# Unit 0 of a rotary embedding kernel: smaller rows for its first half, and GpSimd's queue for its second

## The chip, the cores and the metric

The kernel runs on one core of a Trainium2 chip. The metric is the device time of one execution in microseconds (us). A run more than 1.5% above the fastest of its kernel is called slow. All comparisons below are between the others, called fast, unless a text says otherwise. A profile is one execution, and its span is shorter than its measured time by a nearly constant 1.7 to 1.8 us, so traces are compared with traces and times with times. The profiled execution of the kernel before took 84.54 us (span 82.8 us), which is above its median of 84.26 us, so a difference of a few tenths of a us can't be read from two spans.

## The reference, cut to what matters

```python
angles = np.outer(positions * scale, freqs)
cos, sin = np.cos(angles), np.sin(angles)
x_first, x_second = x[:, :, :, :half], x[:, :, :, half:]      # x: (8, 8, 1024, 64) float32
out_first = x_first * cos - x_second * sin
out_second = x_first * sin + x_second * cos
```

Input and output are 16.8 MB each. Whatever the kernel does, it moves 33.6 MB.

## The kernel before

The 64 heads are worked in four units of 16 heads. A unit is 128 partitions of 32 KB, 4 MB in HBM. GpSimd issues the loads, which cast float32 to float16 on the way; only a quarter of unit 0 is loaded by SyncE, without a cast. VectorE rotates in place in float16, half a unit at a time, ScalarE casts the half to a float32 tile OUT, and OUT is stored. `FIRST` cuts the first half of unit 0 into stores with rows of 4, 4 and 8 KB per partition. A row is what a store takes from one partition; in the traces each row is one packet, and a store's 128 rows are spread over sixteen DMA engines, eight on each.

```python
FIRST = (0, NH // 4, NH // 2, NH)          # NH = 4096 elements, 16 KB: half a unit's row
xout = ctx.enter_context(tc.tile_pool(name="xout", bufs=3))
...                                         # loads of X0..X3 from GpSimd, sine and cosine tables
for u in range(NU):
    OUT = xout.tile([P, N], FP32, tag="O")
    for s in range(2):
        ...                                 # four VectorE instructions on X[u], in place
        pin(nc.scalar.copy(out=OUT[:, ns], in_=Xf[u][:, ns]))
        if u in (0, NU - 1):
            eng = nc.gpsimd if (u, s) == (NU - 1, 0) else nc.sync
            cuts = FIRST if (u, s) == (0, 0) else (ns.start, ns.stop)
            for a, b in zip(cuts, cuts[1:]):
                pin(eng.dma_start(out=ov[u][:, a:b], in_=OUT[:, a:b]))
    if u not in (0, NU - 1):
        pin(nc.gpsimd.dma_start(out=ov[u], in_=OUT))
```

## Time and profile before

| | kernel before |
|---|---|
| time, median | 84.26 us (3 runs, 84.17 to 84.31) |
| span of the profile | 82.8 us |
| busy: VectorE, ScalarE, GpSimd | 60.3, 38.5, 5.2 us |
| DMA engines, mean share from 2.0 to 81.2 us | 1.00 |
| last instruction of VectorE, last cast of ScalarE end | 69.8 us, 73.5 us |
| last store issued, landed | 73.5 us, 81.9 us |

To read it: an engine with 73% of the span (VectorE) looks like the bound, and it is not. What matters is that the sixteen DMA engines are busy throughout from 2.0 to 81.2 us (mean share 1.00). The page's list of DMA issues shows who issues what (KB of each, then median us from issue to landing):

```profile
out_dram<-OUT POOLq DMA_DIRECT2D x2, 4096.0 KB, 14.7
...
out_dram<-OUT SPq DMA_DIRECT2D x2, 2048.0 KB, 18.0
...
out_dram<-OUT SPq DMA_DIRECT2D x2, 512.0 KB, 17.6
out_dram<-OUT SPq DMA_DIRECT2D x1, 1024.0 KB, 23.0
```

SyncE (SP) stores unit 0 in two stores of 512 KB, one of 1 MB and one of 2 MB, and the last half of unit 3. GpSimd (POOL) stores units 1 and 2 and the first half of unit 3. A store of 512 KB alone would take 1.3 us (8 rows of 0.16 us on each engine); that it needs 17.6 us to land tells that it shares every DMA engine with the loads.

### The profile page before, as it was taken

The page shows a single profiled execution, that of the slowest core. Times are in us where ns is not written, and L with a number is a line of the kernel's source. Part 1 is how long each engine was busy: PE and PEld are TensorE (multiplying, and loading weights), DVE is VectorE, ACT ScalarE, POOL GpSimd, SP SyncE. Part 2 cuts the span into 40 slices and gives each one's busy share as a digit, 9 for nine tenths or more (in the row PEclk, how much of TensorE's full clock was granted, in tenths as well). Part 3 has the DMA queues.
Part 4 walks back from the last instruction along what each step waited for, and adds up shares of the span by engine and source line. Part 5 has one row for each costly group of instructions (what it writes and reads, how often), then busy time and mean ns, then how long its engine had stood idle before and what let it go on. Part 6 is the DMA issues. An engine that isn't in the chain of part 4 may idle for free.

```text
span 82.8 us, 181 instructions
## 1 busy us (share of the span) xinstructions
PE 6.5 (8%) x18; PEld 2.6 (3%) x18; DVE 60.3 (73%) x40; ACT 38.5 (47%) x18; POOL 5.2 (6%) x15
## 2 busy tenths in 40 slices
PE   0011798200000000000000000000000000000000
PEld 0011233000000000000000000000000000000000
DVE  0306276999999999999999999999999997000000
ACT  1402259992960691294088049209606912950000
POOL 4920000000000000000000200000100020000000
PEclk9999999997555555555555555555555555555555
DMA  2898997999799799899898999997999899799990
GB/s 44 343 314 190 238 261 158 230 253 214 166 253 245 166 277 230 196 279 253 190 158 360 447 443 420 515 499 309 459 491 428 348 507 459 317 443 420 443 443 8
DMA packets 2018, 25.70 MB, mean 310 GB/s; under 512 B 354, under 2 KB 354, under 8 KB 610
## 3 DMA queue, kind: packets, MB, share of 16 engines
q0 software_dynamic: 1008, 18.35, 75.0%
q1 hardware_dynamic: 864, 7.34, 21.6%
q10 hardware_dynamic: 146, 0.01, 0.1%
HBM read 16.79 MB, written 16.78 MB: 405 GB/s over the span
## 4 chain that ended last, share of the span: by engine, by line
DVE 63%; ACT 7%; DMA 6%; issue 5%; PE 5%; DVEq 1%; ACTq 0%
DVE X L154 22%; DVE pr L153 22%; DVE X L158 10%; DVE X L155 8%; DMA freq_row<-in_freqs_dram 6%; ACT OUT L161 4%; PE ps L129 4%; DVEq L197 1%; ACT T L139 1%; PE cfreq L97 1%; ACT tab L122 1%; DVE r L113 1%; DVE y L104 1%; ACTq L70 0%; ACT tab L117 0%
## 5 line engine op out<-in xcount | busy, mean ns | idle before, releaser
L161 ACT CAST OUT<-X 128x4096 f32<-128x4096 f16 x8 | 28.8, 3605 | 25.8 <-DVE X L158 25.8
L153 DVE TENSOR_TENSOR pr<-X,T 128x4096 f16<-128x4096 f16 x8 | 18.3, 2292 | 1.0 <-ACT T L139 0.7
L154 DVE TENSOR_TENSOR X<-X,T 128x4096 f16<-128x4096 f16 x8 | 18.3, 2292 | 0.3
L155 DVE TENSOR_TENSOR X<-X,pr 128x2048 f16<-128x2048 f16 x8 | 9.8, 1225 | 0.3
L158 DVE TENSOR_TENSOR X<-pr,X 128x2048 f16<-128x2048 f16 x8 | 9.7, 1218 | 0.0
L139 ACT CAST T<-ps 128x1024 f16<-128x1024 f32 x6 | 5.7, 1028 | 2.6 <-PE ps L129 2.6
L129 PE MATMUL ps<-tab,sel 128*128 128x512 f16 x16 | 5.9, 534 | 2.6 <-ACT tab L122 2.2
L168 POOL DMA_DIRECT2D out_dram<-OUT x2 | 1.1, 536 | 54.5 <-ACT OUT L161 54.5
L137 DVE CAST T<-ps 128x1024 f16<-128x1024 f32 x2 | 2.4, 1224 | 2.2 <-PE ps L129 2.2
L95 DVE COPY sel<-one 128x2048 f16<-128x2048 f16 x1 | 0.7, 695 | 2.8 <-POOL one L87 2.8
L117 ACT ACTIVATE tab<-r 128x256 f16<-128x256 f32 x1 | 0.4, 416 | 4.8 <-DVE r L113 4.8
L129 PEld LDWEIGHTS <-sel 128*128 128x128 f16 x16 | 2.1, 130 | 6.0 <-issue 5.6
L117 ACT ACT_TABLE_LOAD x1 | 1.3, 1283 | 1.7 <-issue 1.7
L92 POOL DMA_DIRECT2D X<-in_x_dram x3 | 2.0, 659 | 0.0
L140 ACT CAST X<-X0f 128x2048 f16<-128x2048 f32 x1 | 1.9, 1942 | 0.0
L100 DVE CAST posf<-pos_i 128x8 f32<-128x8 int32 x1 | 0.2, 171 | 2.2 <-DMA pos_i<-in_positions_dram 2.2
L97 PE MATMUL cfreq<-freq_row,coef 1*128 1x32 f32 x2 | 0.6, 390 | 5.9 <-DMA freq_row<-in_freqs_dram 5.9
L166 POOL DMA_DIRECT2D out_dram<-OUT x1 | 0.5, 531 | 6.6 <-ACT OUT L161 6.6
L104 DVE TENSOR_TENSOR y<-posf,cfreq 128x256 f32<-128x256 f32 x1 | 0.4, 421 | 0.7 <-PE cfreq L97 0.7
L83 POOL DMA_DIRECT2D X<-in_x_dram x1 | 0.7, 669 | 0.8 <-POOLq L183 0.8
L97 PEld LDWEIGHTS cfreq<-freq_row,coef 1*128 1x128 f32 x2 | 0.5, 304 | 5.9 <-issue 5.9
L122 ACT ACTIVATE tab<-ra,quarter 128x256 f16<-128x256 f32 x1 | 0.5, 508 | 0.0
(11 smaller groups left out, 2.3 us busy)
## 6 DMA issues: line engine op xcount, KB each, us to landing
out_dram<-OUT POOLq DMA_DIRECT2D x2, 4096.0 KB, 14.7
X<-in_x_dram POOLq DMA_DIRECT2D x3, 2048.0 KB, 29.2
out_dram<-OUT SPq DMA_DIRECT2D x2, 2048.0 KB, 18.0
out_dram<-OUT POOLq DMA_DIRECT2D x1, 2048.0 KB, 10.3
X<-in_x_dram POOLq DMA_DIRECT2D x1, 1536.0 KB, 11.5
X0f<-in_x_dram SPq DMA_DIRECT2D x1, 1024.0 KB, 4.8
out_dram<-OUT SPq DMA_DIRECT2D x2, 512.0 KB, 17.6
out_dram<-OUT SPq DMA_DIRECT2D x1, 1024.0 KB, 23.0
```

Of the source, the lines that this page charges most:

```text
L92: pin(nc.gpsimd.dma_start(out=Xf[u], in_=xv[u]))
L97: nc.tensor.matmul(out=cfreq, lhsT=coef, rhs=freq_row, start=True, stop=True)
L117: pin(nc.scalar.activation(out=tab[:, 0], in_=r, func=AF.Sin, bias=0.0, scale=-_TWO_PI_DN))
L129: nc.tensor.matmul(out=ps[:, i].rearrange("p t w -> p (t w)"), lhsT=sel[:, g + i].rearrange("s h q -> s (h q)"), rhs=tab.rearrange("s t k ...
L137: pin(nc.vector.tensor_copy(out=dst, in_=ps))
L139: pin(nc.scalar.copy(out=dst, in_=ps))
L140: pin(nc.scalar.copy(out=Xf[0][:, N - Q :], in_=X0f[:, :Q]))
L153: pin(nc.vector.tensor_tensor(out=pr, in0=Xs, in1=sin_b, op=ALU.mult))
L154: pin(nc.vector.tensor_tensor(out=Xs, in0=Xs, in1=cos_b, op=ALU.mult))
L155: pin(nc.vector.tensor_tensor(out=Xs[:, :, 0, :], in0=Xs[:, :, 0, :], in1=pr[:, :, 1, :], op=ALU.subtract))
L158: pin(nc.vector.tensor_tensor(out=Xs[:, :, 1, :], in0=pr[:, :, 0, :], in1=Xs[:, :, 1, :], op=ALU.add))
L161: pin(nc.scalar.copy(out=OUT[:, ns], in_=Xf[u][:, ns]))
```

## The change

Its intent is to give SyncE's stores of unit 0 shorter rows, so that they take less of the DMA engines from the loads, and to move half of unit 0 out of SyncE's queue, so that it does not compete with the store of unit 1.

```diff
-    FIRST = (0, NH // 4, NH // 2, NH)
+    C1 = NH // 4
...
-            if u in (0, NU - 1):
-                eng = nc.gpsimd if (u, s) == (NU - 1, 0) else nc.sync
-                cuts = FIRST if (u, s) == (0, 0) else (ns.start, ns.stop)
-                for a, b in zip(cuts, cuts[1:]):
-                    pin(eng.dma_start(out=ov[u][:, a:b], in_=OUT[:, a:b]))
-        if u not in (0, NU - 1):
+            if (u, s) == (0, 0):
+                for c in range(0, NH, C1):
+                    pin(nc.sync.dma_start(out=ov[u][:, c : c + C1], in_=OUT[:, c : c + C1]))
+            if u == NU - 1:
+                eng = nc.sync if s else nc.gpsimd
+                pin(eng.dma_start(out=ov[u][:, ns], in_=OUT[:, ns]))
+        if u == 0:
+            OUT0 = OUT
+        elif u < NU - 1:
             pin(nc.gpsimd.dma_start(out=ov[u], in_=OUT))
+        if u == 1:
+            pin(nc.gpsimd.dma_start(out=ov[0][:, NH:], in_=OUT0[:, NH:]))
```

## The prediction

> **What bounds the kernel now.** I began with the page's chain of work that ended last. It names VectorE for 63% of the span, and it ends at the last cast on ScalarE (69.87 us, 3.60 us long), nine microseconds before the end of the span. The chain therefore stops where the final store begins, and says nothing about how long that store waits. So I went to the DMA lines next, first of the page and then of the windows view over stretches of the span (columns: stretch and its length, busy us of each engine with its instruction count, TensorE clock, DMA share, GB/s written).
>
> ```profile
> DMA  2898997999799799899898999997999899799990
> ...
> q0 software_dynamic: 1008, 18.35, 75.0%
> q1 hardware_dynamic: 864, 7.34, 21.6%
> ...
> HBM read 16.79 MB, written 16.78 MB: 405 GB/s over the span
> ```
> ```profile
> 2.00:81.20 79.20, 6.46 (x18) 2.57 (x18) 60.30 (x40) 38.25 (x18) 4.21 (x10) 0.61 1.00 323
> 24.00:44.60 20.60, 0.00 (x0) 0.00 (x0) 20.29 (x13) 10.21 (x4) 0.00 (x0) 0.50 1.01 229
> 44.60:50.00 5.40, 0.00 (x0) 0.00 (x0) 5.33 (x4) 1.96 (x2) 0.54 (x1) 0.50 1.03 437
> 76.00:80.00 4.00, 0.00 (x0) 0.00 (x0) 0.00 (x0) 0.00 (x0) 0.00 (x0) 0.50 1.03 442
> ```
>
> From 2.0 to 81.2 us the mean busy share of the 16 DMA engines is 1.00. (The page's 7s are an effect of booking a packet to the slice in which it starts.) The kernel is bound by its transfers from the first load to the last store: 33.6 MB in 79.2 us is 424 GB/s. The 229 GB/s of the load stage is the same rate, because a load's float32 rows are counted as float16 when written. The list of VectorE's waits has none for a load of X, and its last wait ends at 13.4 us. So a change pays only if it shortens packets or the time in which the DMA engines have none. What is not bound by DMA is only the first 2.0 us and the last 1.6 us.
>
> The order of the transfers is read from the DMA view in short windows: q1 is SyncE's queue, q0 GpSimd's.
>
> ```profile
> q1 hardware_dynamic: 76, 0.31, 101.5%
> ```
> ```profile
> q1 hardware_dynamic: 142, 1.68, 104.1%
> ```
> ```profile
> q0 software_dynamic: 16, 0.52, 186.6%
> q1 hardware_dynamic: 1, 0.02, 5.9%
> ```
> ```profile
> 45.58 0.54 POOL L168 DMA_DIRECT2D out_dram<-OUT  x1 [40.90 <-ACT OUT L161]
> ```
>
> The first is 43.9 to 44.65 us, where the loads have ended and SyncE's 4 KB rows run alone. The second is 46.12 to 49.9 us: GpSimd has finished issuing the store of unit 1 (45.58 + 0.54, last fence, from the timeline), yet for 3.8 us every packet is still SyncE's. The third is 49.95 to 50.6 us: the first sixteen 32 KB rows of unit 1, one on each engine. So SyncE's stock of unit 0 is what keeps the engines busy between the end of the loads (about 44.7 us) and the start of unit 1's store (about 50.2 us). This is the stretch that the change touches.
>
> **What the Trainium skill says.** "DMA: Bandwidth & Descriptors", Specifications, gives a fabric ceiling of 435 GB/s; the trace agrees (437 and 442 GB/s in the windows above). Its section Queues, rings and completion order says that each DMA engine goes round-robin between queues at packet granularity. The trace agrees: from 28.0 to 31.2 us the DMA view counts 48 packets of q0 and 38 of q1, so about one 4 KB row passes for each 32 KB row loaded. Its section Rules for kernel authors says that spreading transfers over issuing engines gives no bandwidth; that is what I expect of the move to GpSimd's queue in itself. Specifications puts the first byte at about 1 us after a GpSimd issue and 0.6 us after a SyncE issue. The trace agrees on SyncE (the first load's issue ends at 1.12 us, no packet before 1.7 us, nine by 1.9 us) but not on GpSimd, as I work out next.
>
> **The delay of a new queue.** SyncE's first store was issued by 24.45 us and has no packet before 27.7 us; its last one was issued by 73.83 us and has none before 75.95 us. With 0.6 us of its own that leaves about 2.7 us behind 32 KB loads (1.23 us each) and 1.5 us behind 16 KB rows (0.61 us each): some 2.4 packets of the other queue are always taken first. For unit 1 the mean wait is 50.2 - 46.12 = 4.1 us; less 2.4 x 0.61 = 1.5 us, GpSimd's own delay is about 2.6 us. The very first load gives a bound: its issue ends at 1.93 us and its packets begin at 4.65 to 5.2 us, at most 2.7 us to the earliest, and part of that is waiting behind SyncE's load. I take 2.4 us, between 1.7 and 2.7.
>
> **The change part by part.**
> 1. Two 512 KB stores with 4 KB rows replace one 1 MB store with 8 KB rows. From the fence of 43.9 to 44.65 us a 4 KB row alone takes 1.015 x 0.75 x 16 / 76 = 0.160 us, and among loads (28.0 to 31.2 us, 12.8% for 38) 0.172 us. An 8 KB row takes 0.308 us (44.9 to 46.9 us: 106 packets, two of them semaphores, 100.0%). Each engine has 8 rows of 8 KB or 16 of 4 KB: 16 x 0.160 - 8 x 0.308 = 0.10 us, up to 0.29 us. I take +0.15 us. Nothing changes before 44.7 us, for the rows that pass among the loads are the same 4 KB ones in both kernels. SyncE's extra issue (about 0.35 us) lies on an idle engine.
> 2. The second half of unit 0, 2 MB, leaves SyncE's queue at 31.3 us and is issued by GpSimd just after unit 1, near 46.1 us, behind it in the same queue. Its work is the same: eight 16 KB rows an engine, 4.9 us. What changes is the stock. At 44.7 us SyncE now has only 16 rows x 0.16 = 2.6 us left and is empty at 47.3 us, while the first packet of unit 1 can come at 46.12 + 2.4 = 48.5 us. All sixteen engines then stand idle for about 1.2 us (0.5 to 1.5 us for the range of the delay, and up to 2.9 us if the 50.2 us of before are all delay). Later stages are full to the end, so this is never regained: +1.2 us.
> 3. Buffers. Unit 3's output takes the buffer of unit 0's, so its first cast must wait for the late half: unit 1 runs 48.5 to 58.2 us (8 rows x 1.21), the half to 63.1 us, and lands about 0.7 us later (SyncE's second store landed at 45.5 us, its rows were through by 44.8 us), at 63.8 to 64.2 us. The cast would start at 62.86 us: about 1.2 us late. That costs nothing: ScalarE idles 3.40 us before the last cast at 69.87 us, so that one is not moved, and unit 3's first store, issued at about 68 us and ready near 71 us, is queued before unit 2's rows run out at about 72.8 us.
>
> Sum: 84.26 + 0.15 + 1.2 = 85.6; I shade it to 85.5 us, because the delay with an idle queue may be below what I inferred from a full one.
>
> **Rivals.**
> - GpSimd's delay is as short as the skill's 1 us. Then unit 1 begins before 47.3 us, there is no hole and the time is 84.3 to 84.5 us. Against it: 3.8 us without a packet in the second window above.
> - The delay is a fixed 4 us whatever is in front of it. The hole is 2.9 us and the time about 87.3 us. Against it: the first load, whose packets came by 2.7 us.
> - The buffer wait becomes the bound: if the late half landed after 66.3 us (69.87 less a cast of 3.60), the last cast and store would slip too. Another 2 us of delay would be needed. Even then the stock of unit 2 covers it, so the time is at most some tenths worse.
> - Shorter rows and less in SyncE's queue let the loads or unit 1 through earlier. For it: GpSimd's rows no longer alternate with SyncE's from 50 to 57 us, so unit 1 lands earlier. But VectorE waits for no load and ScalarE for no store, and total packet time is unchanged, so this gives 84.3 us, not less. I see no term that lowers the sum.
>
> **Range and chances.** The low end, 84.5 us, is a hole of almost nothing with the row cost; the high end, 86.3 us, is a hole of 1.9 us. The 2% line lies at 85.95 us, which needs a hole above 1.5 us: about one chance in five. Faster by 2% would need shorter packets; 3% for something unseen.
>
> **What would show it.** In the changed trace I expect DMA share 1.00 up to about 47 us, a stretch near 47.3 to 48.5 us with no packets (an idle slice in the DMA row), then only q0 until SyncE's last store at about 76 us; 512 packets of 4 KB in all, 32 an engine, where there were 256; the first cast of unit 3 waiting for a DMA for about a microsecond; the last cast still at about 69.9 us; the last packets at about 82.4 us. I am wrong if the hole is absent, if GpSimd's first packet comes before 47.3 us or after 50 us, or if the last cast slips.

## The result, and the profile after

The changed kernel takes 84.50 us (median of 6 runs, 84.39 to 84.58), the kernel before 84.27 us in the same rounds. The ratio is 1.0026, with a 95% interval of 1.0013 to 1.0039. A ratio is the mean time of one kernel's fast runs over that of the other's in the same rounds, so it is not quite the ratio of the medians. The change costs about 0.2 us; by the 2% mark of these comparisons the two are the same. The prediction was 85.5 us.

First the page of the changed kernel, then the windows view over two of the stretches that the prediction shows of the kernel before.

```profile
DMA  3798896996999798799798997997999799699990
...
q0 software_dynamic: 1152, 20.45, 80.8%
q1 hardware_dynamic: 864, 5.24, 16.1%
...
HBM read 16.79 MB, written 16.78 MB: 405 GB/s over the span
```
```profile
2.00:81.20 79.20, 6.73 (x18) 2.67 (x18) 60.31 (x40) 38.25 (x18) 4.74 (x11) 0.59 1.01 323
44.60:50.00 5.40, 0.00 (x0) 0.00 (x0) 5.33 (x4) 1.96 (x2) 1.07 (x2) 0.50 1.13 479
```

Two megabytes have moved from q1 (SyncE) to q0 (GpSimd), as intended. But the DMA engines are as full as before: 1.01 over the same 79.2 us, and the stretch that I expected to have a hole, 44.6 to 50.0 us, is full as well. Next, the DMA view in three short windows: 43.9 to 44.65 us, 46.12 to 46.65 us, and 46.65 to 47.4 us, and then GpSimd's timeline from 44 to 48 us.

```profile
q1 hardware_dynamic: 86, 0.30, 99.3%
```
```profile
q1 hardware_dynamic: 52, 0.21, 97.5%
```
```profile
q0 software_dynamic: 16, 0.52, 162.6%
q1 hardware_dynamic: 52, 0.15, 48.9%
```
```profile
45.58 0.54 POOL L171 DMA_DIRECT2D out_dram<-OUT  x1 [40.89 <-ACT OUT L161]
46.10 0.54 POOL L173 DMA_DIRECT2D out_dram<-OUT  x1
```

GpSimd issues unit 1 at the same instant as before, but its first sixteen rows come between 46.65 and 47.4 us, 3.3 us earlier than in the kernel before, and just as SyncE's last rows run out. In the packet records the first of them starts at 46.70 us, 0.58 us after the end of the issue. The last packets end at 81.54 us, against 81.53 us before. The list of issues has:

```profile
out_dram<-OUT POOLq DMA_DIRECT2D x2, 4096.0 KB, 12.1
...
out_dram<-OUT SPq DMA_DIRECT2D x4, 512.0 KB, 21.1
```

Unit 1 lands 5 us earlier than before (its issue to landing is the larger part of the fall of this median from 14.7 to 12.1 us), which nothing waits for.

### The profile page after: what moved, and what is told of

Its sections match the earlier page's. It is cut to its first block, busy times and chain, and to the rows that moved or that the text cites. A ratio compares the mean times of both kernels' runs of the same rounds, so it can differ in the third digit from the quotient of the medians.

```text
span 82.8 us, 181 instructions
## 1 busy us (share of the span) xinstructions
PE 6.7 (8%) x18; PEld 2.7 (3%) x18; DVE 60.3 (73%) x40; ACT 38.5 (47%) x18; POOL 5.7 (7%) x16
## 4 chain that ended last, share of the span: by engine, by line
DVE 63%; ACT 7%; DMA 6%; issue 5%; PE 5%; DVEq 1%; ACTq 0%
DVE X L154 22%; DVE pr L153 22%; DVE X L158 10%; DVE X L155 8%; DMA freq_row<-in_freqs_dram 6%; ACT OUT L161 4%; PE ps L129 4%; DVEq L204 1%; ACT T L139 1%; PE cfreq L97 1%; ACT tab L122 1%; DVE r L113 1%; DVE y L104 1%; ACTq L70 0%; ACT tab L117 0%
## 5 line engine op out<-in xcount | busy, mean ns | idle before, releaser
L171 POOL DMA_DIRECT2D out_dram<-OUT x2 | 1.1, 538 | 53.9 <-ACT OUT L161 53.9
L167 POOL DMA_DIRECT2D out_dram<-OUT x1 | 0.5, 533 | 6.6 <-ACT OUT L161 6.6
L173 POOL DMA_DIRECT2D out_dram<-OUT x1 | 0.5, 541 | 0.0
## 6 DMA issues: line engine op xcount, KB each, us to landing
out_dram<-OUT POOLq DMA_DIRECT2D x2, 4096.0 KB, 12.1
```

## The experiments

Theory 1, the prediction's: GpSimd needs 2.4 us from the end of an issue to the first packet. Theory 2, formed after the result: it needs about 0.6 us, and the 4 us in the kernel before were SyncE's own rows, already queued on each engine ahead of unit 1. A third question is where the remaining 0.2 us come from: the shorter rows, the queue, or something else. Twelve kernels ran; all gave correct results. "Before" in the same rounds had medians of 84.31 to 84.37 us.

| run | what differs | median us | ratio to before (95%) |
|---|---|---|---|
| a_rows_only | 4 KB rows, second half stays with SyncE | 84.83 | 1.0056 (1.0044 to 1.0069) |
| b_queue_only | rows as before, second half to GpSimd | 84.62 | 1.0029 (1.0016 to 1.0042) |
| c_short_stock | SyncE keeps only 1 MB of unit 0 | 86.58 | 1.0262 (1.0248 to 1.0276) |
| d_all_4k | all of unit 0 from SyncE in 4 KB rows | 84.76 | 1.0049 (1.0035 to 1.0063) |
| t_ninth_issue | before, 8 KB rows in two stores of 64 partitions | 85.45 | 1.0136 (1.0121 to 1.0151) |
| a_sixteen_issues | 4 KB rows, second half in eight stores | 93.18 (three of six runs slow; the fast ones 91.82 to 92.75) | 1.0929 (1.0889 to 1.0969) |
| f_one_half | before, first half in one store | 84.28 | 0.9997 (0.9973 to 1.0021) |
| g_whole_unit | before, unit 0 in one store | 84.45 | 1.0035 (1.0010 to 1.0059) |
| e_three_quarters | SyncE keeps 1.5 MB of unit 0 | 85.31 | 1.0106 (1.0085 to 1.0127) |
| c_early_unit1 | short stock, unit 1 in two halves, the first early | 84.42 | 1.0004 (0.9991 to 1.0018) |
| h_one_half_moved | the change, first half in one store | 84.51 | 1.0019 (1.0005 to 1.0033) |
| after_again | the change once more | 84.53 | 1.0020 (1.0007 to 1.0034) |

### GpSimd's delay by itself: c_short_stock

```diff
-                for c in range(0, NH, C1):
+                for c in range(0, NH // 2, C1):
...
-            pin(nc.gpsimd.dma_start(out=ov[0][:, NH:], in_=OUT0[:, NH:]))
+            pin(nc.gpsimd.dma_start(out=ov[0][:, NH // 2 :], in_=OUT0[:, NH // 2 :]))
```

(This edit and the two like it further down are against the changed kernel.)

> Only 1 MB of unit 0 stays with SyncE, the other 3 MB go behind unit 1, so that the engines are empty from about 44.6 us until unit 1 comes, and GpSimd's own delay is seen by itself. Theory of the prediction (2.4 us after the end of the issue at 46.1 us): first packet at 48.5 us, hole 3.9 us, about 88.2 us. Rival (0.6 us): first packet at 46.7 us, hole about 2.1 us, about 86.4 us. If the kernel is not bound by its transfers after all: 84.3 us. Unit 0 lands after 63 us here, so the first cast of unit 3 should wait for a DMA; if such a wait costs nothing, the last cast still starts at 69.9 us.

Measured: 86.58 us. The windows view from 44 to 48 us in steps of 1 us (the last two numbers are DMA share and GB/s; a packet counts in the window in which it starts):

```profile
44.00:45.00 1.00, 0.00 (x0) 0.00 (x0) 0.98 (x1) 1.00 (x1) 0.00 (x0) 0.50 0.09 33
45.00:46.00 1.00, 0.00 (x0) 0.00 (x0) 1.00 (x1) 0.30 (x1) 0.41 (x1) 0.50 0.00 0
46.00:47.00 1.00, 0.00 (x0) 0.00 (x0) 0.97 (x2) 0.00 (x0) 0.66 (x2) 0.50 1.26 524
47.00:48.00 1.00, 0.00 (x0) 0.00 (x0) 1.00 (x2) 0.00 (x0) 0.00 (x0) 0.50 0.48 197
```

Here is the hole that the prediction looked for: SyncE's last row ends at 44.46 us and there is no packet until 46.70 us. And here the delay can be read without anything in front of it. The timeline of GpSimd and the DMA view from 46.65 to 47 us:

```profile
45.59 0.54 POOL L171 DMA_DIRECT2D out_dram<-OUT  x1 [40.91 <-ACT OUT L161]
```
```profile
q0 software_dynamic: 16, 0.52, 360.7%
```

The issue ends at 46.13 us and the first packet starts at 46.70 us, so the delay is 0.57 us (1.11 us from the start of the issue), the number of theory 2. Theory 1's 48.5 us and 88.2 us are out. The run also confirms that the kernel is bound by its transfers: 2.24 us without packets cost 2.21 us of time. That the two numbers are so close is partly chance. Followed engine by engine (the trace names no engine; each packet is put on the one that had just come free), the mean engine stood idle for some 2.7 us, had slightly less packet time in all (0.16 us), and ended its last packet 2.4 us later than in the kernel before; the engine that ends last ended 2.1 us later (83.62 against 81.52 us).

The timeline of ScalarE in this run has one more thing to see:

```profile
62.87 3.61 ACT L161 CAST OUT<-X 128x4096 f32<-128x4096 f16 x1 [3.48 <-DVE X L158]
```

The three quarters of unit 0 landed only at 64.43 us, yet unit 3's first cast began at 62.87 us and had waited for VectorE alone. It does not reuse unit 0's buffer. The addresses in the compiled programs say why: before, unit 3's OUT lies at unit 0's address; where unit 0 is held longer, as in the change, it is given unit 1's.

### Half as much taken away: e_three_quarters

```diff
-                for c in range(0, NH, C1):
+                for c in range(0, 3 * NH // 4, C1):
...
-            pin(nc.gpsimd.dma_start(out=ov[0][:, NH:], in_=OUT0[:, NH:]))
+            pin(nc.gpsimd.dma_start(out=ov[0][:, 3 * NH // 4 :], in_=OUT0[:, 3 * NH // 4 :]))
```

> Three of the four 512 KB stores stay with SyncE, the fourth joins the half behind unit 1. If unit 1 can start 0.57 us after its issue (46.7 us) on engines that have nothing else, SyncE's stock here ends near 45.8 us on the average engine, so a hole of 0.8 to 1.0 us, about 85.3 us: between the change (no hole) and the run with two stores (2.3 us), in proportion to the bytes taken away. If the delay depends on something else, the time does not lie on this line.

Measured: 85.31 us. The same two windows as above, 45 to 47 us:

```profile
45.00:46.00 1.00, 0.00 (x0) 0.00 (x0) 1.00 (x1) 0.24 (x1) 0.47 (x1) 0.50 0.77 315
46.00:47.00 1.00, 0.00 (x0) 0.00 (x0) 0.97 (x2) 0.00 (x0) 0.59 (x2) 0.50 1.26 524
```

SyncE's last row ends at 46.04 us (on most engines before 46 us, hence the 0.77), and the first row of unit 1 starts at 46.63 us, 0.56 us after its issue ended at 46.07 us: the same delay again. The step from this run to the short stock is 512 KB, which is 8 rows of 0.16 us on each engine, 1.27 us; the medians differ by 86.58 - 85.31 = 1.27 us (they are of different rounds and chips; taken over the kernel before in the same rounds, 2.21 - 0.97 = 1.24 us). Going back from this run by the same step gives the slack of the change: 1.27 us less the loss of about 0.8 us here (85.31 us against the change's 84.53 us in the same rounds) is some 0.5 us. By this estimate the change keeps the DMA engines full by half a microsecond of rows, and with half a store less for SyncE it would have begun to lose time.

### Giving the lost time back: c_early_unit1

```diff
-            if u == NU - 1:
-                eng = nc.sync if s else nc.gpsimd
+            if u in (1, NU - 1):
+                eng = nc.sync if (u, s) == (NU - 1, 1) else nc.gpsimd
...
-        elif u < NU - 1:
+        elif 1 < u < NU - 1:
```

(against c_short_stock)

> As the short stock run (86.6 us), but unit 1 is stored in two halves, the first issued by GpSimd near 38.5 us, while the loads still run. If the 2.3 us lost there were the idle engines before unit 1 and nothing else, they come back: 84.3 to 84.6 us, no stretch without packets, although unit 0's three quarters still land late and unit 3's first cast may still wait. If the late landing or the shorter SyncE queue cost the time, it stays at 86.6 us.

Measured: 84.42 us, ratio 1.0004. Everything that the short stock lost is back, with unit 0 still late and still in GpSimd's queue. The windows of 44 to 46 us:

```profile
44.00:45.00 1.00, 0.00 (x0) 0.00 (x0) 1.00 (x1) 1.00 (x1) 0.00 (x0) 0.50 1.13 479
45.00:46.00 1.00, 0.00 (x0) 0.00 (x0) 1.00 (x1) 0.00 (x1) 0.70 (x2) 0.50 1.04 442
```

So the late unit 0 and the shorter SyncE queue cost nothing, and a store issued earlier, while the loads run, removes the loss. Not all of it need have been the idle engines: the short stock also had 0.41 us an engine of packets longer than usual (see the last run below), and these are gone here too.

### What goes ahead of a newly issued store: d_all_4k

```diff
-                cuts = FIRST if (u, s) == (0, 0) else (ns.start, ns.stop)
+                cuts = range(ns.start, ns.stop + 1, NH // 4) if u == 0 else (ns.start, ns.stop)
```

(against the kernel before)

> All of unit 0 on SyncE in eight stores of 4 KB rows. What is ahead of unit 1 on each engine when it is issued is then many small packets. If a fixed number of about 7 packets goes first (0.159 us each), unit 1's first packet comes near 47.8 us; if a fixed time does, near 50 us as before; if a fixed number of bytes (about 100 KB an engine), near 50.7 us; if all that SyncE has queued goes first, not before 52 us. Time by row overhead alone: 16 x 0.159 - 8 x 0.308 = 0.08 us, and 32 x 0.159 - 8 x 0.611 = 0.20 us, so about 84.55 us.

Measured: 84.76 us. The DMA view from the end of GpSimd's issue, 45.87 us, to 49.7 us, and from 49.7 to 50.4 us:

```profile
q1 hardware_dynamic: 444, 1.60, 102.0%
```
```profile
q0 software_dynamic: 16, 0.52, 173.3%
q1 hardware_dynamic: 20, 0.07, 25.7%
```

Unit 1's first packet starts at 49.74 us, 3.9 us after its issue ended; before it was 50.0 us, also 3.9 us after. In the kernel before, 142 of SyncE's packets started in that time, here 444. Their number is not what is fixed, so both my "2.4 packets" and the seven that I tried next are wrong. The bytes are nearly equal (1.60 and 1.68 MB, about 100 KB on each engine), and so is the time. Less the 0.57 us of GpSimd itself, about 3.3 us of SyncE's rows go first, where SyncE has as much. Whether it is a time or a number of bytes that is fixed, these two runs can't tell, since their rows move at nearly the same rate. Two runs further down can, because some of their rows took much longer: in t_ninth_issue unit 1's first packet came 4.31 us after its issue ended, with 1.78 MB started before it, and in a_sixteen_issues (a slow run) 5.55 us after, with 1.75 MB. So the time is not fixed, and the bytes nearly are: 1.60 to 1.78 MB in all four. That SyncE's own new stores waited 2.7 us behind loads, and at the end only as long as rows were left, is of the same kind; no run tests whether the amount is the same in that direction. The time of this run lies 0.4 us above before; 0.24 us of it is explained under the ninth issue.

### Rows or queue: a_rows_only and b_queue_only

```diff
-    FIRST = (0, NH // 4, NH // 2, NH)
+    FIRST = (0, NH // 4, NH // 2, 3 * NH // 4, NH)
```

> Only the rows change: the last 1 MB of the first half goes in two stores of 4 KB rows, the second half stays on SyncE. If the measured +0.2 us of the change is row overhead, this shows most of it: 16 rows of 0.159 us for 8 of 0.308 us on each engine is +0.08 us, so a ratio of about 1.001. If the rows cost nothing, 1.000; if they are the whole of it, 1.0026.

```diff
-                for c in range(0, NH, C1):
-                    pin(nc.sync.dma_start(out=ov[u][:, c : c + C1], in_=OUT[:, c : c + C1]))
+                for c, e in ((0, C1), (C1, 2 * C1), (2 * C1, NH)):
+                    pin(nc.sync.dma_start(out=ov[u][:, c:e], in_=OUT[:, c:e]))
```

(the first against the kernel before, the second against the changed one)

> Only the queue changes: the first half keeps its 4, 4 and 8 KB rows on SyncE, the second half goes to GpSimd behind unit 1. Theory of the prediction (GpSimd's own delay is 2.4 us): first packet of unit 1 at 48.5 us, a hole of about 1.2 us, ratio 1.014. Rival (the delay is at most 0.6 us, and the 4 us of the kernel before were SyncE packets already queued on each engine): first packet right after SyncE's last, near 47.2 us, no hole, ratio 1.000 to 1.002.

Measured: 84.83 us and 84.62 us. The queue alone has no hole (unit 1 starts at 46.90 us) and gives the whole 0.2 us of the change: theory 2 again. The rows alone are slower than rows and queue together, which neither theory allowed. Their trace shows that it is not the rows. The last packet ends at 81.37 us, even earlier than the 81.53 us of the kernel before, but the span ends 1.67 us after it, not 1.24 us. SyncE's stores, with ScalarE's two small loads and the first load of x, take their completion semaphores from eight in rotation. This run is the first with a ninth issue, so the last store has the first semaphore of the eight. At the end SyncE goes through the eight in a fixed order, about 0.06 us each, and only then ends the program: seven waits were still to come after the last store had landed, in the kernel before none. That is 0.43 us of the 0.47 us. Rows themselves: the second 256 rows of 4 KB took 2.54 us an engine in the changed kernel, the 128 rows of 8 KB 2.47 us before. That is +0.07 us.

### The ninth issue: t_ninth_issue and a_sixteen_issues

```diff
                 for a, b in zip(cuts, cuts[1:]):
-                    pin(eng.dma_start(out=ov[u][:, a:b], in_=OUT[:, a:b]))
+                    for h in range(2) if b - a == NH // 2 else (None,):
+                        ps = slice(None) if h is None else slice(h * P // 2, (h + 1) * P // 2)
+                        pin(eng.dma_start(out=ov[u][ps, a:b], in_=OUT[ps, a:b]))
```

> The 8 KB rows of the first half go in two stores of 64 partitions each instead of one of 128: same rows, same queue, but nine issues by SyncE and ScalarE instead of eight. In the run with changed rows alone, the ninth issue came back to the first of eight semaphores, and SyncE's list of final waits, which goes through the eight in order at about 0.06 us each, then had seven still to pass after the last store had landed. If that is what made that run slow, this one is slow too: about +0.4 us, ratio 1.004 to 1.005, with the span's end 1.65 us after the last packet instead of 1.25. If the rows made it slow, 1.000.

```diff
-    FIRST = (0, NH // 4, NH // 2, NH)
+    FIRST = (0, NH // 4, NH // 2, 3 * NH // 4, NH)
...
                 for a, b in zip(cuts, cuts[1:]):
-                    pin(eng.dma_start(out=ov[u][:, a:b], in_=OUT[:, a:b]))
+                    n = 8 if (u, s) == (0, 1) else 1
+                    for h in range(n):
+                        ps = slice(h * P // n, (h + 1) * P // n)
+                        pin(eng.dma_start(out=ov[u][ps, a:b], in_=OUT[ps, a:b]))
```

(both against the kernel before)

> Changed rows as in the run with changed rows alone, and in addition the second half of unit 0 in eight stores of 16 partitions, so that there are sixteen issues and the last store has the last semaphore of the list again. If the list of final waits is the cause, more issues make it faster: the row overhead of 0.08 us remains, ratio 1.001. If the number of stores costs time, slower than the 1.0056 of that run.

Measured: 85.45 us and 93.18 us. In the first, the span ends 1.67 us after the last packet, as expected, so the 0.43 us of the ninth issue are there a second time, and d_all_4k with twelve issues and four waits to come has 1.48 us, which is its 0.24 us. But the run is 1.1 us slower, not 0.4 us: the last packet comes at 82.21 us, 0.7 us late, and the three engines that end last each had one or two 8 KB rows of 0.67 to 0.89 us instead of 0.309 us (eleven of the 128 rows took over 0.5 us; why is not shown). I had taken a split by partitions for free. The second run failed as a test: SyncE must wait for an earlier store to land before it can use its semaphore again (13.4 us of such waits), and many of its 16 KB rows were far longer than 0.611 us, up to 4.1 us, so that the packets took 86.0 us an engine against 80.1 us. Unit 0 landed at 69.7 us and unit 1 at 72.1 us; unit 3's first cast, which in this program has unit 1's buffer, waited for unit 1 until 72.2 us. That more issues can be faster is therefore not shown; that the list of final waits costs 0.06 us for each place is read from three traces (seven, seven and four places), not varied by a run that changes nothing else.

### Larger rows, to beat both: f_one_half, g_whole_unit, h_one_half_moved

```diff
-    FIRST = (0, NH // 4, NH // 2, NH)
+    FIRST = (0, NH)
```

> The first half of unit 0 in one store with 16 KB rows from SyncE, else as before. The path is the packets of the DMA engines: 16 rows of 0.168 and 8 of 0.308 us on each engine become 8 of 0.611 us, so -0.27 us, ratio 0.997, with no wait on the loads: X3 lands some 2.5 us later, near 47.5 us, and is needed only at 55.8 us. If only the last stores matter, 1.000; if the delayed loads matter, above 1.

```diff
-            if u in (0, NU - 1):
+            if u == NU - 1:
...
-        if u not in (0, NU - 1):
-            pin(nc.gpsimd.dma_start(out=ov[u], in_=OUT))
+        if u < NU - 1:
+            pin((nc.gpsimd if u else nc.sync).dma_start(out=ov[u], in_=OUT))
```

> Unit 0 in one store with 32 KB rows from SyncE after both halves are cast, else as before. 8 rows of 1.213 us on each engine for 16 x 0.168 + 8 x 0.308 + 8 x 0.611 us: -0.34 us, ratio 0.996. Unit 1's first packet after a stock of large rows: if about 3.3 us of queued work goes first, near 50 us; if seven packets do, near 52 us. X3 lands near 50 us, still before it is needed at 55.8 us. Issues by the hardware queues are fewer, which the final waits should not show.

```diff
-                for c in range(0, NH, C1):
-                    pin(nc.sync.dma_start(out=ov[u][:, c : c + C1], in_=OUT[:, c : c + C1]))
+                pin(nc.sync.dma_start(out=ov[u][:, :NH], in_=OUT[:, :NH]))
```

(the first two against the kernel before, the third against the changed one)

> The change with the first half in one store of 16 KB rows instead of four of 4 KB rows. On each engine 8 x 0.611 for 32 x 0.164 us: -0.35 us if rows alone count, about 84.1 us, which would beat both kernels. Risk: 16 KB rows pass among the loads four times as fast, so SyncE's stock is gone before the loads end, near 47 us; unit 1 follows in the loads' own queue from 46.7 us, so at most 0.1 us is empty. If no packet time is saved, 84.5 us.

Measured: 84.28, 84.45 and 84.51 us; none beats the kernel before. The first has two kinds of run, three at 84.05 to 84.13 us and three at 84.43 to 84.63 us, so its interval holds 1. In its profile, which is one of the slower kind, the packets took 80.07 us an engine in all, exactly as in the kernel before: the 0.27 us saved in row overhead came back as packets longer than the shortest of their size, mostly in the first 50 us. Two of the six runs of the whole unit took 84.92 and 85.04 us. In its trace unit 1 followed the loads in GpSimd's own queue, so it says nothing of what goes ahead of a newly issued store; that was a poor design of mine.

### The change again: after_again

> The change itself again, on the same chip as the runs beside it. If its +0.2 us is real, the ratio is again 1.001 to 1.004; packets after 44 us should again take 0.1 to 0.3 us an engine more than their shortest time, as in the other runs with unit 0 in GpSimd's queue, and in none with it in SyncE's.

Measured: 84.53 us, ratio 1.0020. The 0.2 us are real. They can't be read from the spans (82.8 us before and after), since the profiled execution of the kernel before was itself 0.3 us above its median. What the traces show beside them is packets after 44 us that take longer than the shortest of their size (1.213 us for 32 KB, 0.611 us for 16 KB). Summed per engine this is 0.23 and 0.21 us in the two profiles of the change, 0.19 us in b_queue_only, 0.25 us in h_one_half_moved (without its loads), 0.39 and 0.41 us in the runs with a hole. It is 0.005 us or less in the kernel before, a_rows_only and d_all_4k, and 0.000 us in c_early_unit1. For example, unit 2's rows take 1.227 us in the change and 1.213 us before, long after everything else is alike. GpSimd's queue as such is not the cause, for c_early_unit1 has three quarters of unit 0 in it. I thought that engines which start their rows in step hinder each other, but the runs with a hole, where all sixteen start within 0.13 us, have no more of it in unit 2 than the change, with 0.34 us. So the longer packets go with the 0.2 us, but that they make it up is not shown by an experiment, and their own cause stays open.

## Why the prediction was wrong, point by point

**What bounds the kernel: right.** Taking packets away from the engines for 2.24 us cost 2.21 us, and filling the stretch again gave it back.

**The delay of a new queue: the step that failed.** The prediction says "For unit 1 the mean wait is 50.2 - 46.12 = 4.1 us; less 2.4 x 0.61 = 1.5 us, GpSimd's own delay is about 2.6 us". GpSimd's own delay measures 0.57 us, twice. The other 3.3 us were SyncE's rows: from the end of the issue on, about 100 KB of them went first on each engine. The 2.4 packets came from two waits of SyncE's stores behind GpSimd's rows, and I carried the number over to the reverse case and to other row sizes; the run with 4 KB rows shows some 24 of them an engine ahead of unit 1. The bound from the first load was misread as well: its rows started where SyncE's rows ended, which is what any delay below 2.7 us would give.

**The hole: not there.** Its term was 48.5 - 47.3 = 1.2 us. With the measured delay unit 1 is ready at 46.7 us, while SyncE's rows last until 46.7 us on the first engine and 47.3 us on the last. What waits behind a queue waits less when that queue is short: the shorter stock, which was to make the hole, is also what let unit 1 in early. The rival with the skill's 1 us, 84.3 to 84.5 us, was the right one; I rejected it for the 3.8 us without a packet of q0, in which every packet was one of q1 and the engines were busy. That its range just reaches the measured 84.50 us is partly luck, for it had no more of the unforeseen 0.2 us than my own sum.

**The rows: right in kind, small.** Predicted +0.15 us, measured +0.07 us an engine; between b_queue_only and the change no difference in time can be seen.

**Buffers: wrong premise, right conclusion.** Unit 3 takes unit 1's buffer in the changed program, so no cast waits; the last cast starts at 69.86 us, as predicted. The wait that was argued to cost nothing never came, so that argument is untested.

**The sum.** With the measured terms it is 84.26 + 0.07 + 0 = 84.33 us. The other 0.2 us I had not foreseen. They go with slightly longer packets in the second half, whose cause is open.

## What to carry to other kernels

When a new transfer starts late, ask what the DMA engines did in the meantime: if they were busy with another queue, the wait may be that queue's stock and not the issuer's latency, and then it shrinks with the stock. Measure an issuer's latency only on engines that have nothing to do. A transfer may be moved to a later queue without leaving the engines idle as long as what remains covers the time until the first packet of the later issue; here the cover was half a microsecond, and one 512 KB store less cost 0.8 us.

## What the Trainium skill lacked or had wrong

- "DMA: Bandwidth & Descriptors", Specifications, first-byte latency: its 1 us for GpSimd is right if counted from the start of the issue (1.11 us measured; 0.57 us from its end), and my prediction wrongly called it too short. Its 0.6 us for SyncE is right only if counted from the end: the first load's issue runs from 0.74 to 1.12 us and its first packet starts at 1.75 us, 1.0 us from the start and 0.63 us from the end. The page does not say from where it counts; counted alike, the two queues were equally quick here.
- The same page, Queues, rings and completion order: packets do alternate between queues, but only after what the other queue had ready. It has no figure for this; here it was about 100 KB an engine from the end of GpSimd's issue (1.60 to 1.78 MB over the sixteen), with 4 KB rows and with 8 and 16 KB rows alike; at the usual rate that took 3.9 us, 0.57 us of it GpSimd's own.
- No page has the completion semaphores of SyncE's and ScalarE's transfers in a rotation of eight, waited for in a fixed order at the end: 0.06 us for each place after the last store's, up to 0.43 us.
